# Half-array products of two heads issued in turns, each head to its own bank, in a hybrid transformer block

## The chip, the cores and the metric

One core of one Trainium2 chip runs the whole program in one launch. The metric is the device time of one execution in microseconds (us); the kernel before has a median of 3474.94 us over three runs (3471.09 to 3478.48).

## The reference, cut to what matters

512 tokens of width 1024, all in float32. A first block of two layers, each: gated feed-forward, a mixer, gated feed-forward. A second block of two layers: gated linear attention (GLA) or sparse attention (NSA), each with a convolutional feed-forward. The change touches three places:

```
def _rwkv7_scan(r, w, k, v, kk, a):          # mixer, 6 heads of 64
    def step(state, inp):
        sa = jnp.einsum('bhij,bhj->bhi', state, a_t)
        state = state * w_t + sa * b_t + v_t * k_t
        y_t = jnp.einsum('bhij,bhj->bhi', state, r_t)
...
def _dilated_attention(q, k, v, slopes, window, dilation):   # mixer, 6 heads of 64
    s = jnp.einsum('bnqchd,bnkchd->bnqchk', qb, kb)
    s = jnp.where(valid, s + bias, -jnp.inf)
    p = jnp.exp(s - logsumexp(s));  o = einsum(p, vb)
...
# GLA, 4 heads with keys of 64: score of a query t and a key s is
#   sum over c of q[t,c] * k[s,c] * exp(sum of the log gates of c from s+1 to t)
```

The mixer joins RWKV, dilated attention and a convolution over 31 taps, and projects the result with `w_out`.

## The kernel before

A projection (`gemm`, lines 261 to 272) multiplies 128 output features by 512 tokens: 8 blocks of the inner width, three TensorE products each (high by high, high by low, low by high), 24 products of 128x512 into one bank. `load_w` brings the weights (SP queue), ACT makes the high part (L258), DVE the low part (L259).

Heads go in pairs: two heads of 64 stand in the lower and the upper 64 partitions of a tile, so a product over the 64 channels of one head uses 64 rows of the array. A product of float32 is written to the queue once and shows in the trace as two records.

PSUM is handed out by name, in the program's order of allocation (`BANKS`):

```
BANKS = {"mm": 2, "rr": 1, "rx": 1, "rz": 1, "at": 2, "po": 1}
```

"mm" serves the projections of the mixer from the seventh on. A tile of a name waits until the tile that had its buffer is read out. The mixer (`mixer`) drives seven generators, `r0` to `r2` (RWKV pairs, with the banks rr, rz and rx), `a0` to `a2` (dilated pairs, bank at) and `c` (the convolution, bank mm), by the list `MIXER`, which lets `c`, `a0`, `a1`, `a2` make all their allocations up to their ends in part before `r0` reaches its scores; then it lets `mem_kv` (8 projections to 256 tokens, bank mm) follow as `tail`. A scheduler of the framework then sets each engine's order from dependences and priorities; the engines run their orders strictly one after the other.

An RWKV pair (`rwkv_pair`): projections, gates, then the scores (L572: for each head, two tiles of four 128x128 products, masked by DVE to SA and SR at L574 and L575), a DMA of SA to DRAM and back (L576, L584), a solve of 15 steps on POOL (L615, L616), a copy (L617), DMAs out and back (L618, L628), the matrices ZD (L634), pM (L637), three iterations (L649, L650), W (L657), G (L666), H (L672), a scan of 7 chunks (L683, L684), the output (L690, L693), the group norm (L696 to L706), transposes (L712) and the gate (L716 to L718). The key transposes are L622.

A dilated pair (`dilated_pair`, `causal_pair`): four query blocks i = 3 to 0, for each head one product of 64x(128(i+1)) (L799), softmax (L731, L732), transposes (L743), products with the values (L749).

GLA (`gla_pair`): for two heads, four diagonal score blocks (L1024), then nine levels with four (two in level 7) products of 128x128 per head (L1047), merged by DVE (L1050) or copied by ACT (L1053). `stream_pair` (NSA) shares `causal_pair`.

Of the kernel before, what the change touches and what calls it, by code (L numbers as in the profile page):

```python
# [13 lines left out]
AF = mybir.ActivationFunctionType  # L14
OP = mybir.AluOpType
# [3 lines left out]
T = 512  # L19
# [167 lines left out]
class Net:  # L187
# [306 lines left out]
    def rwkv_pair(self, l, i, win, xs, R, shared, out):  # L494
# [24 lines left out]
        a = self.s([128, T], "rate")  # L519
# [23 lines left out]
        AR = [self.s([128, 4, 2, 64], "AR") for _ in range(2)]  # L543
        BK = [self.s([128, 4, 2, 64], "BK") for _ in range(2)]
# [20 lines left out]
        SA = [self.s([128, 8, 64], "SA") for _ in range(2)]  # L565
        SR = [self.s([128, 8, 64], "SR") for _ in range(2)]
        wide = lambda name: self.c(name).unsqueeze(1).broadcast_to((128, 4, 64))
        for h in range(2):
            for u in range(2):
                p = self.ps([128, 4, 2, 64])  # L570
                for j in range(4):
                    self.T.matmul(p[:, j].rearrange("p a t -> p (a t)"), BK[u][hb[h], j].rearrange("p a t -> p (a t)"),  # L572
                                  AR[u][hb[h], j].rearrange("p a t -> p (a t)"), start=True, stop=True)
                self.V.tensor_tensor(SA[h][:, h4[u]], p[:, :, 0], wide("strict"), OP.mult)  # L574
                self.V.tensor_tensor(SR[h][:, h4[u]], p[:, :, 1], wide("incl"), OP.mult)  # L575
            self.S.dma_start(dN[h], SA[h][hb[h]])  # L576
        yield

# [17 lines left out]
        for u in range(2):  # L596
            p = self.ps([128, 4, 128])
            for j in range(4):
                n = 4 * u + j
# [16 lines left out]
            self.G.tensor_tensor(Z[:, 0, 0:t, t:16], Z[:, 0, 0:t, t:16], tmp[:, 0:t, 0:nt], OP.add)  # L616
        self.V.tensor_copy(Z[:, 1], Z[:, 0].rearrange("p r t -> p t r"))  # L617
        self.S.dma_start(dZ, Z)  # L618
        for h in range(2):
            pB = self.ps([128, 8, 64])  # L620
            for n in range(8):
                self.T.transpose(pB[:, n], BK[n // 4][hb[h], n % 4].rearrange("p a t -> p (a t)"), self.ident[hb[h], hb[h]])  # L622
            self.A.activation(Bt[h], pB, AF.Copy)
        yield
        C2 = self.s([128, 2, 8, 16], "C2")
        for w in range(2):
# [108 lines left out]
    def causal_pair(self, score, V, tables, z, po, heap):  # L735


        def second(i, P):
            PT = []
            for h in range(2):  # L740
                pt = self.ps([128, (i + 1) * 128])
                for b in range(i + 1):
                    self.T.transpose(pt[:, b * 128:(b + 1) * 128], P[h][:, b * 128:(b + 1) * 128], self.ident)  # L743
                t = self.s([128, (i + 1) * 128], "sm_pt", heap=heap)
                self.A.activation(t, pt, AF.Copy)
                PT.append(t)
            for b in range(i + 1):
                for h in range(2):
                    self.T.matmul(po[64 * h:64 * h + 64, i * 128:(i + 1) * 128], V(h, b), PT[h][:, b * 128:(b + 1) * 128],  # L749
                                  start=b == 0, stop=b == i)  # L750

        tab = [self.s([128, T], "tab", heap=heap) for _ in range(2)]
        for h in range(2):
            self.S.dma_start(tab[h], tables[h])
        last = None
        for i in (3, 2, 1, 0):
            n = (i + 1) * 128
            P = []
            for h in range(2):
                ps = self.ps([128, n])  # L760
                score(ps, h, i)
                P.append(self.softmax(ps, tab[h][:, T - n:T], n, z[:, i, h:h + 1], heap))
            if last:
                second(*last)
            last = i, P
            yield
        second(*last)
        yield

    def dilated_pair(self, l, i, win, xs, R, out):  # L770

        qkv = []
        for w in range(3):
            ps = self.proj(win[10 + 3 * w + i], xs)
            f = self.s([128, T], "aq")
            self.V.tensor_tensor(f, ps, R, OP.mult)
            qkv.append(f)
        q, k, f = qkv
        yield
        pss = self.ps([128, 4, 4])  # L780
        for w in range(2):
            sq = self.s([128, T], "asq", heap="ap")
# [12 lines left out]
        yield  # L795

        def score(ps, h, i):
            b = slice(64 * h, 64 * h + 64)
            self.T.matmul(ps, q[b, i * 128:(i + 1) * 128], k[b, 0:(i + 1) * 128], start=True, stop=True)  # L799
# [197 lines left out]
    def gla_pair(self, i, win, xs, R, low, mk, Vk, rr, out):  # L997
# [19 lines left out]
        self.V.tensor_tensor(k, ps, R, OP.mult)  # L1017
        yield
        S = [self.s([128, 4, 128], "gS") for _ in range(2)]
        for h in range(2):  # L1020
            p = self.ps([128, 4, 128])
            for j in range(4):
                tj = slice(j * 128, (j + 1) * 128)
                self.T.matmul(p[:, j], k[hb[h], tj], q[hb[h], tj], start=True, stop=True)  # L1024
            self.V.tensor_tensor(S[h], p, self.ident.unsqueeze(1).broadcast_to((128, 4, 128)), OP.mult)
        far = [[None, None], [None, None]]
        for lv in range(9):
            n = 1 << lv
            eq = self.s([128, T], "geq")
            self.A.activation(eq, g, AF.Exp)  # L1030
            self.V.tensor_tensor(eq, eq, q, OP.mult)
            if lv == 0:
                ek = k
            else:
                gv = g.rearrange("p (b c) -> p b c", c=n)
                ek = self.s([128, T], "gek")
                self.G.tensor_tensor(ek.rearrange("p (b c) -> p b c", c=n), gv[:, :, n - 1:n].broadcast_to((128, T // n, n)), gv, OP.subtract)
                self.A.activation(ek, ek, AF.Exp)
                self.V.tensor_tensor(ek, ek, k, OP.mult)
            if lv < 8:  # L1040
                gw = g.rearrange("p (b w c) -> p b w c", w=2, c=n)
                self.V.tensor_tensor(gw[:, :, 1], gw[:, :, 1], gw[:, :, 0, n - 1:n].broadcast_to((128, T // (2 * n), n)), OP.add)
            for h in range(2):
                pairs = {7: ((0, 1), (2, 3)), 8: ((0, 2), (0, 3), (1, 2), (1, 3))}.get(lv, ((0, 0), (1, 1), (2, 2), (3, 3)))
                p = self.ps([128, len(pairs), 128])
                for u, (s, t) in enumerate(pairs):
                    self.T.matmul(p[:, u], ek[hb[h], s * 128:(s + 1) * 128], eq[hb[h], t * 128:(t + 1) * 128], start=True, stop=True)  # L1047
                if lv < 7:
                    m = mk[lv // 4][:, (lv % 4) * 128:(lv % 4 + 1) * 128].bitcast(I32)
                    self.V.copy_predicated(S[h], m.unsqueeze(1).broadcast_to((128, 4, 128)), p)  # L1050
                else:
                    far[h][lv - 7] = self.s([128, len(pairs), 128], "gfar")
                    self.A.activation(far[h][lv - 7], p, AF.Copy)  # L1053
            yield
        for h in range(2):
            hd = 2 * i + h
# [200 lines left out]
    def stream_pair(self, u, st, q, K, V, gates, O, bank):  # L1257
# [3 lines left out]
        po = self.ps([128, T], bank)  # L1261
        g = u // 2

        def score(ps, h, i):
            for w in range(2):
                self.T.matmul(ps, q[h][:, i * 128:(i + 1) * 128], K[g][w][:, 0:(i + 1) * 128], start=w == 0, stop=w == 1)
# [245 lines left out]
```

## Time and profile before

| what | value |
|---|---|
| median of three runs | 3474.94 us |
| the profiled execution | 3467.64 us |
| its span, first to last instruction | 3464.6 us |
| TensorE (PE) busy | 3419.1 us, 99% of the span |
| VectorE (DVE) busy | 1748.7 us, 50% |
| ScalarE (ACT) busy | 1232.1 us, 36% |
| GpSimd (POOL) busy | 538.8 us, 16% |
| mean granted TensorE clock | 0.996 of full speed |

The profiled execution stands 3.0 us above its span and 7.3 us below the median. PE's busy time counts a product until its modelled end, so the spacing of starts, and not the mean duration, tells what one costs.

### The profile page before, as it was taken

To read this page: it belongs to the slowest core of one execution; us is meant where nothing else is said; L and a number is where in the kernel's file an instruction comes from. 1 tells how busy PE (TensorE), PEld (TensorE's weight loads), DVE (VectorE), ACT (ScalarE), POOL (GpSimd) and SP (SyncE) were. 2 spreads that over 40 slices of the span, in tenths; PEclk is the share of its full clock that TensorE was granted. 3 is DMA by queue.
4 is the path that set the end of the run, shared out by engine and by line. 5 is a ranking of instruction groups with operands and counts; after the bars stand their busy time and mean duration, and the time that the engine had idled before them with its cause. 6 is when DMAs were issued, how large, how long until landed. Compare 5 with 4: busy or idle time off the path is not lost.

```text
span 3464.6 us, 43276 instructions
## 1 busy us (share of the span) xinstructions
PE 3419.1 (99%) x17126; PEld 2729.0 (79%) x17126; DVE 1748.7 (50%) x2857; ACT 1232.1 (36%) x1946; POOL 538.8 (16%) x509
## 2 busy tenths in 40 slices
PE   8999999999999999999999999999999999999998
PEld 6888777878888888877778888777888887778886
DVE  5333498663333433359765333385655354465532
ACT  3222334442222322233444222343433244643332
POOL 2110025011111111012401110020211000211100
PEclk9999999999999999999999999999999999999999
DMA  4223322132233223322123223322322333132232
GB/s 138 94 92 109 101 85 64 40 126 95 94 91 98 91 97 93 109 94 78 54 96 106 94 95 103 110 68 70 107 92 96 106 121 97 49 98 94 97 91 80
DMA packets 127593, 321.55 MB, mean 93 GB/s; under 512 B 32384, under 2 KB 34976, under 8 KB 127392
## 3 DMA queue, kind: packets, MB, share of 16 engines
q1 hardware_dynamic: 127392, 318.80, 29.0%
q8 instruction: 134, 2.20, 0.3%
q14 instruction: 67, 0.55, 0.0%
HBM read 303.81 MB, written 14.94 MB: 92 GB/s over the span
## 4 chain that ended last, share of the span: by engine, by line
PE 94%; DVE 3%; POOL 1%; DMA 1%; issue 1%; ACT 0%; SPq 0%; DVEq 0%; POOLq 0%; ACTq 0%
PE mm L272 13%; PE mm L270 13%; PE mm L271 13%; PE at L271 8%; PE at L270 8%; PE at L272 8%; PE rr L272 4%; PE rr L271 4%; PE rr L270 4%; PE rx L272 3%; PE rx L270 3%; PE rx L271 3%; PE po L749 1%; PE at L799 1%; PE at L743 1%
## 5 line engine op out<-in xcount | busy, mean ns | idle before, releaser
L258 ACT ACTIVATE whi<-raw 128x1024 fp32r<-128x1024 f32 (+2 forms) x566 | 562.6, 995 | 1685.2 <-issue 528.8
L259 DVE TENSOR_TENSOR wlo<-raw,whi 128x1024 fp32r<-128x1024 f32 (+2 forms) x566 | 650.7, 1150 | 502.0 <-ACT whi L258 486.2
L270 PE MATMUL mm<-xh,whi 128*128 128x512 f32 x1216 | 485.1, 399 | 9.1 <-ACT whi L258 9.0
L272 PE MATMUL mm<-xh,wlo 128*128 128x512 f32 x1216 | 487.5, 401 | 0.0
L271 PE MATMUL mm<-xl,whi 128*128 128x512 f32 x1216 | 484.7, 399 | 0.8 <-DVE xl L347 0.7
L272 PE MATMUL at<-xh,wlo 128*128 128x512 f32 x736 | 291.3, 396 | 0.0
L270 PE MATMUL at<-xh,whi 128*128 128x512 f32 x736 | 291.1, 395 | 0.0
L271 PE MATMUL at<-xl,whi 128*128 128x512 f32 x736 | 291.0, 395 | 0.0
L373 POOL TENSOR_TENSOR fg<-fg,bR 128x512 f32<-128x512 f32 x88 | 155.2, 1765 | 806.6 <-ACT fg L372 806.6
L270 PEld LDWEIGHTS mm<-xh,whi 128*128 128x128 f32 x1216 | 228.9, 188 | 65.1 <-ACT whi L258 9.5
L272 PEld LDWEIGHTS mm<-xh,wlo 128*128 128x128 f32 x1216 | 228.7, 188 | 60.6 <-issue 3.9
L271 PEld LDWEIGHTS mm<-xl,whi 128*128 128x128 f32 x1216 | 228.7, 188 | 57.3 <-issue 2.5
L270 PE MATMUL mm<-hi,whi 128*128 128x512 f32 x652 | 259.8, 400 | 3.3 <-ACT hi L287 1.5
L271 PE MATMUL mm<-lo,whi 128*128 128x512 f32 x652 | 258.2, 396 | 0.1
L272 PE MATMUL mm<-hi,wlo 128*128 128x512 f32 x652 | 257.5, 396 | 0.0
L331 POOL TENSOR_TENSOR nacc<-nacc,nsq 128x512 f32<-128x512 f32 x70 | 107.0, 1529 | 781.3 <-ACT nsq L330 780.8
L272 PEld LDWEIGHTS at<-xh,wlo 128*128 128x128 f32 x736 | 138.1, 188 | 35.5 <-DVE wl L514 1.5
L271 PEld LDWEIGHTS at<-xl,whi 128*128 128x128 f32 x736 | 138.2, 188 | 34.8 <-issue 1.5
L272 PE MATMUL rr<-xh,wlo 128*128 128x512 f32 x416 | 164.8, 396 | 0.8 <-DVE wlo L259 0.8
L270 PEld LDWEIGHTS at<-xh,whi 128*128 128x128 f32 x736 | 138.2, 188 | 34.1 <-ACT gy L1005 0.8
L271 PE MATMUL rr<-xl,whi 128*128 128x512 f32 x416 | 164.3, 395 | 0.0
L270 PE MATMUL rr<-xh,whi 128*128 128x512 f32 x416 | 164.2, 395 | 0.0
(667 smaller groups left out, 5878.8 us busy)
## 6 DMA issues: line engine op xcount, KB each, us to landing
raw<-ffn_gu SPq DMA_DIRECT2D x176, 512.0 KB
raw<-c_gu SPq DMA_DIRECT2D x88, 512.0 KB
raw<-ffn_dn SPq DMA_DIRECT2D x64, 448.0 KB
raw<-w_in SPq DMA_DIRECT2D x46, 512.0 KB
raw<-ffn_dn SPq DMA_DIRECT2D x32, 512.0 KB
raw<-c_dn SPq DMA_DIRECT2D x32, 448.0 KB
raw<-a_w_in SPq DMA_DIRECT2D x17, 512.0 KB
park<-x SPq DMA_DIRECT2D x32, 256.0 KB
```

Source lines behind the costliest of these rows:

```text
L258: self.A.activation(hi, raw, AF.Copy)
L259: self.V.tensor_tensor(lo, raw, hi.bitcast(F32), OP.subtract)
L270: self.T.matmul(ps, wh, xh, start=first and j == 0, stop=False)
L271: self.T.matmul(ps, wh, xl, start=False, stop=False)
L272: self.T.matmul(ps, wl, xh, start=False, stop=last and j == nk - 1)
L331: self.G.tensor_tensor(acc, acc, sq, OP.add)
L373: self.G.tensor_tensor(g, g, R, OP.mult)
L743: self.T.transpose(pt[:, b * 128:(b + 1) * 128], P[h][:, b * 128:(b + 1) * 128], self.ident)
L749: self.T.matmul(po[64 * h:64 * h + 64, i * 128:(i + 1) * 128], V(h, b), PT[h][:, b * 128:(b + 1) * 128], start=b == 0, stop=b == i)
L799: self.T.matmul(ps, q[b, i * 128:(i + 1) * 128], k[b, 0:(i + 1) * 128], start=True, stop=True)
```

## The change

For two heads whose products use the lower and the upper half of the array, the products are now written in turns, head 0, head 1, head 0, head 1, with both output tiles allocated first. RWKV's scores and key transposes take the second head's tile from "mm". The dilated scores are cut into blocks of 128 keys, in turns by head. In `stream_pair` the products keep their order; only the softmax of the first head is now written after both heads' products.

```diff
-        for h in range(2):
-            for u in range(2):
-                p = self.ps([128, 4, 2, 64])
-                for j in range(4):
-                    self.T.matmul(p[:, j]..., BK[u][hb[h], j]..., AR[u][hb[h], j]..., start=True, stop=True)
-                self.V.tensor_tensor(SA[h][:, h4[u]], p[:, :, 0], wide("strict"), OP.mult)
-                self.V.tensor_tensor(SR[h][:, h4[u]], p[:, :, 1], wide("incl"), OP.mult)
+        for u in range(2):
+            p = [self.ps([128, 4, 2, 64]), self.ps([128, 4, 2, 64], "mm")]
+            for j in range(4):
+                for h in range(2):
+                    self.T.matmul(p[h][:, j]..., BK[u][hb[h], j]..., AR[u][hb[h], j]..., start=True, stop=True)
+            for h in range(2):
+                self.V.tensor_tensor(SA[h][:, h4[u]], p[h][:, :, 0], wide("strict"), OP.mult)
+                self.V.tensor_tensor(SR[h][:, h4[u]], p[h][:, :, 1], wide("incl"), OP.mult)
...
+        pB = [self.ps([128, 8, 64]), self.ps([128, 8, 64], "mm")]
+        for n in range(8):
+            for h in range(2):
+                self.T.transpose(pB[h][:, n], BK[n // 4][hb[h], n % 4]..., self.ident[hb[h], hb[h]])
         for h in range(2):
-            pB = self.ps([128, 8, 64])
-            for n in range(8):
-                self.T.transpose(pB[:, n], BK[n // 4][hb[h], n % 4]..., self.ident[hb[h], hb[h]])
-            self.A.activation(Bt[h], pB, AF.Copy)
+            self.A.activation(Bt[h], pB[h], AF.Copy)
...
-            P = []
-            for h in range(2):
-                ps = self.ps([128, n])
-                score(ps, h, i)
-                P.append(self.softmax(ps, tab[h][:, T - n:T], n, z[:, i, h:h + 1], heap))
+            ps = [self.ps([128, n]) for _ in range(2)]
+            score(ps, i)
+            P = [self.softmax(ps[h], tab[h][:, T - n:T], n, z[:, i, h:h + 1], heap) for h in range(2)]
...
+        def score(ps, i):
+            for j in range(i + 1):
+                for h in range(2):
+                    b = slice(64 * h, 64 * h + 64)
+                    self.T.matmul(ps[h][:, j * 128:(j + 1) * 128], q[b, i * 128:(i + 1) * 128], k[b, j * 128:(j + 1) * 128], start=True, stop=True)
...
+        p = [self.ps([128, 4, 128]) for _ in range(2)]
+        for j in range(4):
+            for h in range(2):
+                self.T.matmul(p[h][:, j], k[hb[h], tj], q[hb[h], tj], start=True, stop=True)
...
+            p = [self.ps([128, len(pairs), 128]) for _ in range(2)]
+            for u, (s, t) in enumerate(pairs):
+                for h in range(2):
+                    self.T.matmul(p[h][:, u], ek[hb[h], s * 128:(s + 1) * 128], eq[hb[h], t * 128:(t + 1) * 128], start=True, stop=True)
```

(The calls are shortened with `...` inside; the last two pieces are GLA's diagonal blocks and levels.) Lines move by 3 to 8: the scores are L573 in the changed kernel, the key transposes L625, pM L641, the dilated scores L804, GLA's levels L1053.

How the order moves on PE, at three places. First place, layer 0 of the mixer: the RWKV scores. Before, while a projection (mm_3016, the tile that `c` uses) runs, the first product group of r0's second head stands in the middle of it:

```order
L441 MATMUL rx_4110<-cpack,ksq_4108 128x2 x2
L572 MATMUL rr_3683<-AR_3638,BK_3640 128x128 x4
L271 MATMUL mm_3016<-xl_2467,whi_3012 128x512
L272 MATMUL mm_3016<-xh_2466,wlo_3013 128x512
L270 MATMUL mm_3016<-xh_2470,whi_3012 128x512
```

Changed, the second head's groups of r0 (mm_3681, mm_3695) and of r1 (mm_3987) stand behind the last projection of the mixer's input, mm_3573; these are the rows at its end:

```order
L272 MATMUL mm_3573<-xh_2470,wlo_3570 128x512
L449 MATMUL at_5102<-cpack,hex_5100 128x128 x4
L449 MATMUL at_5110<-cpack,hex_5108 128x128 x4
L596 MATMUL rr_3735<-cpack,AR_3651 64x128 x4
L573 MATMUL mm_3695<-AR_3651,BK_3653 128x128 x4
L625 MATMUL mm_3811<-cpack,BK_3652 128x64 x4
L625 MATMUL mm_3811<-cpack,BK_3653 128x64 x4
L431 MATMUL at_5116<-cpack,aq_3306 128x128 x4
L804 MATMUL at_5129<-aq_3273,aq_3240 128x128 x4
L603 MATMUL rr_3742<-cpack,shq_2685 64x128 x4
L804 MATMUL at_5130<-aq_3273,aq_3240 128x128 x4
L573 MATMUL mm_3987<-AR_3945,BK_3947 128x128 x4
```

The second head's scores moved from the midst of the projections to their end; the key transposes stand with all of one tile in a row (mm_3811), and the dilated scores with the four blocks of one head together (at_5129, later at_5130).

Second place, the end of the same mixer. Before, projections of `mem_kv` (mm_5752, 256 wide) and already those of `w_out` (mm_5817) stand between the last transposes of the RWKV pairs:

```order
L271 MATMUL mm_5752<-ml_5460,whi_5748 128x256
L272 MATMUL mm_5752<-mh_5459,wlo_5749 128x256
L712 MATMUL rx_4977<-cpack,gn_y_4955 64x128 x4
L938 MATMUL mm_5779<-cpack,mvf_5777 128x128 x2
L270 MATMUL mm_5817<-hi_5801,whi_5820 128x512
L271 MATMUL mm_5817<-lo_5802,whi_5820 128x512
```

Changed, the three pairs end together, and nothing stands between the scan's outputs (L697), the transposes (L716), the gates (L720) and the first product of `w_out`:

```order
L697 MATMUL rz_4853<-rS_4676,Rt_3961 64x64
L716 MATMUL rr_4806<-cpack,gn_y_4729 64x128 x4
L716 MATMUL rx_4989<-cpack,gn_y_4967 64x128 x4
L716 MATMUL rr_4813<-cpack,gn_y_4729 64x128 x4
L716 MATMUL rz_4912<-cpack,gn_y_4887 64x128 x4
L716 MATMUL rx_4996<-cpack,gn_y_4967 64x128 x4
L720 MATMUL rr_4820<-lora_u_2571,lora_w_2576 128x512
L716 MATMUL rz_4919<-cpack,gn_y_4887 64x128 x4
L720 MATMUL rx_5003<-lora_u_2571,lora_w_2576 128x512
L720 MATMUL rz_4926<-lora_u_2571,lora_w_2576 128x512
L270 MATMUL mm_5853<-hi_5837,whi_5856 128x512
```

All of `mem_kv` moved ahead of them. Third place, GLA's level 0. Before, four products of one head and then four of the other:

```order
L271 MATMUL at_17164<-xl_16895,whi_17160 128x512
L1047 MATMUL rx_17612<-geq_17608,gk_17080 128x128 x4
L1047 MATMUL rr_17618<-geq_17608,gk_17080 128x128 x4
L272 MATMUL at_17164<-xh_16894,wlo_17161 128x512
L1024 MATMUL at_17632<-gq_17123,gk_17156 128x128 x4
```

Changed:

```order
L1053 MATMUL rx_17684<-geq_17680,gk_17152 128x128
L1053 MATMUL rr_17685<-geq_17680,gk_17152 128x128
L1053 MATMUL rx_17684<-geq_17680,gk_17152 128x128
L1053 MATMUL rr_17685<-geq_17680,gk_17152 128x128
L1053 MATMUL rx_17684<-geq_17680,gk_17152 128x128
L1053 MATMUL rr_17685<-geq_17680,gk_17152 128x128
L1053 MATMUL rx_17684<-geq_17680,gk_17152 128x128
L1053 MATMUL rr_17685<-geq_17680,gk_17152 128x128
```

Here the two heads do stand in turns. From GLA's output projection to the end of the program PE's order is the same in both kernels, and so it is up to the scores of r0 in layer 0.

## Rows read from the trace of the kernel before

**Rows 1.** The page: busy time by engine, and the chain that ended last

```profile
PE 3419.1 (99%) x17126; PEld 2729.0 (79%) x17126; DVE 1748.7 (50%) x2857; ACT 1232.1 (36%) x1946; POOL 538.8 (16%) x509
...
PE 94%; DVE 3%; POOL 1%; DMA 1%; issue 1%; ACT 0%; SPq 0%; DVEq 0%; POOLq 0%; ACTq 0%
```

**Rows 2.** Busy time by stretch: mixer 0, mixer 1, GLA (columns in the first row)

```profile
core 0: us, PE busy (x) PEld busy (x) DVE busy (x) ACT busy (x) POOL busy (x), PEclk, DMA share, GB/s
...
545.00:708.00 163.00, 156.70 (x1521) 129.45 (x1519) 114.10 (x287) 70.89 (x164) 39.12 (x72) 0.98 0.22 63
1650.00:1814.00 164.00, 157.75 (x1531) 129.29 (x1530) 117.58 (x292) 71.59 (x166) 39.38 (x72) 0.99 0.23 67
2240.00:2400.00 160.00, 157.32 (x867) 123.61 (x866) 116.39 (x208) 75.72 (x137) 29.32 (x24) 0.99 0.21 69
```

**Rows 3.** Timeline of PE: start, us, engine, line, operation, count

```profile
462.25 1.16 PE L572 MATMUL rr<-AR,BK 64*128 64x128 f32 x8
463.33 0.49 PE L272 MATMUL mm<-xh,wlo 128*128 128x512 f32 x1
463.66 0.40 PE L270 MATMUL mm<-xh,whi 128*128 128x512 f32 x1
463.90 0.39 PE L271 MATMUL mm<-xl,whi 128*128 128x512 f32 x1
```

**Rows 4.** Timeline of PE in GLA: two heads' blocks, rx and rr

```profile
2258.18 0.27 PE L1024 MATMUL rx<-gq,gk 64*128 64x128 f32 x1
2258.28 0.27 PE L1024 MATMUL rr<-gq,gk 64*128 64x128 f32 x1
2258.29 0.27 PE L1024 MATMUL rx<-gq,gk 64*128 64x128 f32 x1
```

**Rows 5.** Timeline of PE: r0's third score group, where the two orders part

```profile
477.74 1.16 PE L572 MATMUL rr<-AR,BK 64*128 64x128 f32 x8
```

**Rows 6.** Timelines of DVE and PE: last SA and first pM of r0, r1, r2

```profile
490.46 0.42 DVE L574 TENSOR_TENSOR SA<-rr,cpack 128x256 f32<-128x256 f32 x1
543.76 1.00 PE L637 MATMUL rr<-No,ZD 128*128 128x64 f32 x8
524.99 0.41 DVE L574 TENSOR_TENSOR SA<-rz,cpack 128x256 f32<-128x256 f32 x1
584.54 1.22 PE L637 MATMUL rz<-No,ZD 128*128 128x64 f32 x10
556.05 0.42 DVE L574 TENSOR_TENSOR SA<-rx,cpack 128x256 f32<-128x256 f32 x1
601.31 0.96 PE L637 MATMUL rx<-No,ZD 128*128 128x64 f32 x7 [2.09 <-DVE ZD L634]
```

**Rows 7.** Timeline of POOL: the solve of r0, its first and last step

```profile
512.51 0.21 POOL L615 TENSOR_TENSOR T<-N,Z 64x15 f32<-64x15 f32 x1
529.19 0.21 POOL L616 TENSOR_TENSOR Z<-Z,T 64x15 f32<-64x15 f32 x1
```

**Rows 8.** Timelines of PE and DVE: small products, and a step of the scan

```profile
692.03 0.29 PE L270 MATMUL mm<-mh,whi 128*128 128x256 f32 x1
692.15 0.28 PE L271 MATMUL mm<-ml,whi 128*128 128x256 f32 x1
645.09 0.74 PE L666 MATMUL rx<-BKt,W 64*64 64x64 f32 x18
645.77 1.12 PE L799 MATMUL at<-aq,aq 64*128 64x512 f32 x2
638.26 0.28 DVE L684 TENSOR_SCALAR rS<-rz,ec 128x64 f32<-128x64 f32 x1 [0.35 <-PE rz L672]
```

**Rows 9.** Timelines of DVE and PE: group norm and gate of r2, w_out beside them

```profile
686.20 0.68 DVE L696 TENSOR_REDUCE gn_m<-rx 128x8 f32<-128x512 f32 x1
705.82 0.75 DVE L718 SCALAR_TENSOR_TENSOR bv<-bv,vec,rx 128x512 f32<-128x512 f32 x1 [1.19 <-PE rx L716]
705.72 0.50 PE L271 MATMUL mm<-lo,whi 128*128 128x512 f32 x1
```

More of the change, by code (lines that the diff above doesn't have):

```diff
@@ L567, in rwkv_pair @@
         wide = lambda name: self.c(name).unsqueeze(1).broadcast_to((128, 4, 64))
-        for h in range(2):
-            for u in range(2):
-                p = self.ps([128, 4, 2, 64])
-                for j in range(4):
-                    self.T.matmul(p[:, j].rearrange("p a t -> p (a t)"), BK[u][hb[h], j].rearrange("p a t -> p (a t)"),
-                                  AR[u][hb[h], j].rearrange("p a t -> p (a t)"), start=True, stop=True)
-                self.V.tensor_tensor(SA[h][:, h4[u]], p[:, :, 0], wide("strict"), OP.mult)
-                self.V.tensor_tensor(SR[h][:, h4[u]], p[:, :, 1], wide("incl"), OP.mult)
+        for u in range(2):
+            p = [self.ps([128, 4, 2, 64]), self.ps([128, 4, 2, 64], "mm")]
+            for j in range(4):
+                for h in range(2):
+                    self.T.matmul(p[h][:, j].rearrange("p a t -> p (a t)"), BK[u][hb[h], j].rearrange("p a t -> p (a t)"),
+                                  AR[u][hb[h], j].rearrange("p a t -> p (a t)"), start=True, stop=True)
+            for h in range(2):
+                self.V.tensor_tensor(SA[h][:, h4[u]], p[h][:, :, 0], wide("strict"), OP.mult)
+                self.V.tensor_tensor(SR[h][:, h4[u]], p[h][:, :, 1], wide("incl"), OP.mult)
+        for h in range(2):
             self.S.dma_start(dN[h], SA[h][hb[h]])
@@ L618, in rwkv_pair @@
         self.S.dma_start(dZ, Z)
+        pB = [self.ps([128, 8, 64]), self.ps([128, 8, 64], "mm")]
+        for n in range(8):
+            for h in range(2):
+                self.T.transpose(pB[h][:, n], BK[n // 4][hb[h], n % 4].rearrange("p a t -> p (a t)"), self.ident[hb[h], hb[h]])
         for h in range(2):
-            pB = self.ps([128, 8, 64])
-            for n in range(8):
-                self.T.transpose(pB[:, n], BK[n // 4][hb[h], n % 4].rearrange("p a t -> p (a t)"), self.ident[hb[h], hb[h]])
-            self.A.activation(Bt[h], pB, AF.Copy)
+            self.A.activation(Bt[h], pB[h], AF.Copy)
         yield
@@ L795, in dilated_pair @@
         yield
-        def score(ps, h, i):
-            b = slice(64 * h, 64 * h + 64)
-            self.T.matmul(ps, q[b, i * 128:(i + 1) * 128], k[b, 0:(i + 1) * 128], start=True, stop=True)
+        def score(ps, i):
[3 more added lines that the diff above has]
+                    self.T.matmul(ps[h][:, j * 128:(j + 1) * 128], q[b, i * 128:(i + 1) * 128], k[b, j * 128:(j + 1) * 128], start=True, stop=True)
         yield from self.causal_pair(score, lambda h, b: Vk[:, b, 64 * h:64 * h + 64],
@@ L1019, in gla_pair @@
         S = [self.s([128, 4, 128], "gS") for _ in range(2)]
-        for h in range(2):
[L1021 to L1025, printed above, removed]
+        p = [self.ps([128, 4, 128]) for _ in range(2)]
+        for j in range(4):
+            for h in range(2):
+                tj = slice(j * 128, (j + 1) * 128)
+                self.T.matmul(p[h][:, j], k[hb[h], tj], q[hb[h], tj], start=True, stop=True)
+        for h in range(2):
+            self.V.tensor_tensor(S[h], p[h], self.ident.unsqueeze(1).broadcast_to((128, 4, 128)), OP.mult)
         far = [[None, None], [None, None]]
@@ L1042, in gla_pair @@
                 self.V.tensor_tensor(gw[:, :, 1], gw[:, :, 1], gw[:, :, 0, n - 1:n].broadcast_to((128, T // (2 * n), n)), OP.add)
+            pairs = {7: ((0, 1), (2, 3)), 8: ((0, 2), (0, 3), (1, 2), (1, 3))}.get(lv, ((0, 0), (1, 1), (2, 2), (3, 3)))
+            p = [self.ps([128, len(pairs), 128]) for _ in range(2)]
+            for u, (s, t) in enumerate(pairs):
+                for h in range(2):
+                    self.T.matmul(p[h][:, u], ek[hb[h], s * 128:(s + 1) * 128], eq[hb[h], t * 128:(t + 1) * 128], start=True, stop=True)
             for h in range(2):
[L1044 to L1047, printed above, removed]
                 if lv < 7:
                     m = mk[lv // 4][:, (lv % 4) * 128:(lv % 4 + 1) * 128].bitcast(I32)
-                    self.V.copy_predicated(S[h], m.unsqueeze(1).broadcast_to((128, 4, 128)), p)
+                    self.V.copy_predicated(S[h], m.unsqueeze(1).broadcast_to((128, 4, 128)), p[h])
                 else:
                     far[h][lv - 7] = self.s([128, len(pairs), 128], "gfar")
-                    self.A.activation(far[h][lv - 7], p, AF.Copy)
+                    self.A.activation(far[h][lv - 7], p[h], AF.Copy)
             yield
@@ L1262, in stream_pair, with score @@
         g = u // 2
-        def score(ps, h, i):
-            for w in range(2):
-                self.T.matmul(ps, q[h][:, i * 128:(i + 1) * 128], K[g][w][:, 0:(i + 1) * 128], start=w == 0, stop=w == 1)
+        def score(ps, i):
+            for h in range(2):
+                for w in range(2):
+                    self.T.matmul(ps[h], q[h][:, i * 128:(i + 1) * 128], K[g][w][:, 0:(i + 1) * 128], start=w == 0, stop=w == 1)
         yield from self.causal_pair(score, lambda h, b: V[:, b, 64 * g:64 * g + 64],
```

## The prediction, made before the changed kernel was run

> **What bounds the kernel.** I read the page first: TensorE is busy for 99% of the span, and 94% of the chain that ended last runs through it [rows 1]. So whatever saves PE slots saves time, and whatever leaves PE without work that is ready costs time; no other engine is above 50%. The windows say where there is room: the second half of each mixer leaves PE idle for 163.00 - 156.70 = 6.3 us and 164.00 - 157.75 = 6.25 us, GLA for 160.00 - 157.32 = 2.7 us [rows 2]. In the mixers that density comes from cover: the RWKV pairs run one behind the other, and projections and `mem_kv` fill PE while a pair waits for its solve.
>
> **What a slot costs.** PE's timelines give spacings of starts. A projection product starts 0.24 us after the last one [rows 3]; 0.23 over longer runs of them, which I use. A `mem_kv` product, 256 wide, takes 0.12 [rows 8]. A float32 product leaves two records, and of 128 columns in half the array each takes 0.11: the next rx block starts 0.11 us after the one before [rows 4]. Eight such records keep the projection away for 463.33 - 462.25 = 1.08 us [rows 3], so some 0.1 to 0.2 us of each group is the change of shape; I take 0.1. A 64x64 product takes 0.06 (18 records in 645.77 - 645.09 = 0.68 us, two to a product) [rows 8].
>
> **GLA: the part that does what it says.** The order puts the levels and the diagonal blocks in turns, both banks, rr and rx, being GLA's own. There are 19 pairs of groups of up to 16 records (304 in all: 272 in the levels, 32 on the diagonal). That halves share time is seen already: rr starts at 2258.28 and rx at 2258.29, 0.01 us apart, where a slot is 0.11 [rows 4]. There the program has four products of rx and then four of rr; the last three records of the first head run beside the first three of the second. So a pair of adjacent groups costs 13 slots today, and groups with something between them 16. By the order 10 of the 19 are adjacent: 10 x 13 + 9 x 16 = 274 slots against 19 x 8 = 152. The 122 slots at 0.11 are 13.4 us, and 9 changes of shape less are 0.9: **-14 us**. GLA is 157 of 160 us PE [rows 2], so most of it should reach the end; the bounds are -10 (DVE's merges between levels become the wait; DVE is 116 of 160) and -17. The Trainium skill, "TensorE: Matmul & The Clock Gate", section Part 3: Packing small matmuls, says that matmuls start and end strictly in program order. The overlap above, of a later group with an earlier one, is against it; by that rule all 19 pairs would cost 16 slots now, and GLA would gain 17 us.
>
> **The mixers: the part that doesn't.** In the rows of the changed order, RWKV scores, key transposes and dilated scores still stand grouped by head. The second head's tile comes from "mm" (or is the second "at"), and that tile is not free when the first head's is. "mm" is handed out in the program's order, and the list `MIXER` lets `c` and the dilated pairs allocate ahead of `r0`'s scores. So r0's second head waits for the mixer's last projections, and with it those of r1 and r2: all three solves start late and together. The Trainium skill, "TensorEngine Tiling (Array Packing)", section Gotcha 1: PSUM Pressure, warns of the cause: row tiles must go to different banks. No run here shows that rule by itself, and my sum does not use it.
>
> The path through layer 0, from r0's third score group at 477.74 [rows 5], where the orders part:
>
> 1. To the last input projection the changed order has 332 products: 211 of 512 columns at 0.23 make 49 us; 88 of 128 columns at 0.22, 34 smaller ones and some 20 changes of shape make 26. That is 75 us.
> 2. To r2's second-head scores it has 171: 11 projections (2.5), 91 of 128 (20), 69 smaller (6.5), changes (3): 32 us. So 477.74 + 75 + 32 = 585; I add 4 for waits on DVE's masks and take 589 (585 to 595).
> 3. From the last SA to the first pM (two trips through DRAM, POOL's 15 steps, ZD) the pairs took 53.3, 59.5 and 45.3 us [rows 6]; I take the mean, 53, so pM at 642. The low bound is the fastest. The high one is 66: POOL's loop alone takes 529.19 - 512.51 + 0.21 = 16.9 us [rows 7], the three loops now stand step by step in turns in POOL's order, r2's first step is behind most of r0's and r1's, and SP has r0's last DMAs behind r2's.
> 4. From pM to `w_out` the order has: iterations of all three pairs with the `mem_kv` left (147 products at 0.12 = 18 us, 115 of 128 at 0.22 = 25, smaller ones 9), 52 us and 3 of waits; the scan, 7 chunks, each a product, a step of DVE of 0.28 us after a wait of 0.35 [rows 8], a mask and the way back, some 1 us: 7; 138 products of 64x64 at 0.06: 8; then group norm and gate, with nothing beside them on PE. That took 705.82 + 0.75 - 686.20 = 20.4 us for r2 alone [rows 9]; the three pairs share DVE, so 23 (20 to 29). Together 93 us: **`w_out` starts at 735**.
>
> Before, the end of r2's gate was at 706.57, but 14 products of `w_out` had already run beside it, until 705.72 [rows 9]: the like mark is 705.72 - 14 x 0.23 = 702.5. Layer 0 so loses **32 us** (bounds +14 and +60 from steps 2 to 4). Layer 1 has the same order of things, with the second heads' scores a little earlier against `mem_kv` (86 products after pM, not 151; 65 x 0.12 = 8 us less): **+24 us** (+6 to +52). What is late next is `w_out` and all behind it; from there the orders are alike, and weights for `w_out` stand on SP behind the Z transfers and the stores of `mem_kv`, tens of us ahead of need, so I give them nothing.
>
> The same from the other side: idle. PE's work stays, less 4 to 6 us of shape changes per layer. If the start of the solves leaves 5 us uncovered, the solve 20 (the `mem_kv` before pM covers little of 53), the scan 5 and the group norm 15, a mixer idles 45 us against 6.3 now [rows 2]: +39, less 5, +34. The two ways agree within a few us.
>
> **Small edits.** Dilated scores in blocks: two records of 512 columns end after 1.12 us [rows 8], eight of 128 after 1.16 [rows 3], so 0.04 for each of 30 such products: +1 us, hidden in the above. `stream_pair`'s later softmax: its order on PE is unchanged; nothing (-1 to +1, by GLA's 2.7 us of idle as the nearest like stretch).
>
> **Sum:** +32 + 24 - 14 = **+42 us**. The sum is made on the profiled execution (3467.64, 3.0 above its span); the median is 7.3 above that. I add it to the median: 3474.94 + 42 = **3517 us**.
>
> **Rivals.**
>
> *A. Everything goes in turns as written.* Then L572 (6 pairs, 32 records each; half of 192 slots at 0.11 is 11 us), the transposes (half of 192 at 0.03: 3) and the dilated scores (6 pairs, 10 blocks, 2 heads, 2 records; half at 0.11: 13) are saved too: -41 in all, **3434**. Against it: the order shows none of the three in turns. Chance 0.03.
>
> *B. The delay of the solves is hidden, faster.* If each solve finishes with its cover still running, only GLA counts: -14, **3461**. For it: POOL, SP and ACT have slack [rows 1]. Against it: it decides at a solve shorter than the work in front of pM, and the order has 40 `mem_kv` products there, 5 us, and some 25 us of other work, against 53 [rows 6]. Chance 0.05.
>
> *C. The three solves get in each other's way.* If POOL's loops run one after another behind r2's start, two more loops of 16.9 us [rows 7] come in front of pM, some 25 us after what overlaps, in each layer: 3517 + 50 = **3567**. Chance 0.13. For it: the loops stand step by step in turns.
>
> *D. About even.* Losses at their low bounds (14 + 6) and GLA's gain: within 10 us of before, **3480**. Chance 0.1, the half of it within 0.2%.
>
> The forecast has 0.69. A measurement of this kernel can tell about 0.2%, 7 us. Faster by more: A, B, a little of D, 0.07; within: 0.06; slower: 0.87. The range leaves out A and B and the far end of C: 3474 to 3572.
>
> **What would show it.** In the profile after: idle of 35 to 60 us in each mixer on PE, released by POOL's ZD (L637 in the changed numbering), by DVE in the scan (L687) and in the group norm; r2's last SA near 589 and the first product of `w_out` near 735; starts of rx and rr within 0.01 us all through L1053, GLA some 14 us shorter; scores at L573 not in turns. It is wrong if idle in the mixers stays below 15 us, or if PE runs L573 or L804 in turns after all.

## The result, and the profile after

The changed kernel takes 3503.22 us (median of four runs, 3498.31 to 3504.49) against 3476.71 for the kernel before, run beside it. The medians stand 26.5 us apart; the ratio is 1.0086, 95% interval 1.0072 to 1.0099, which is some 30 us. Below, differences between whole runs go by the ratios, and differences between stages by the profiles. Forecast were +42 us, a range of 3474 to 3572, and 0.87 for slower. The sign, the place and GLA's gain in the middle of a loss came as forecast; the sizes of three terms did not.

The page of the changed kernel, the rows that answer to [rows 1]:

```profile
PE 3426.5 (98%) x17270; PEld 2750.0 (79%) x17270; DVE 1733.6 (49%) x2857; ACT 1228.0 (35%) x1946; POOL 506.0 (14%) x509
...
PE 94%; DVE 4%; ACT 1%; issue 1%; POOL 0%; DMA 0%; SPq 0%; DVEq 0%; POOLq 0%; ACTq 0%
```

The mean granted clock fell from 0.996 to 0.985. Both kernels have long runs of projections in the same order, so the time can be laid out by stage: from the first input projection of a mixer to the first projection of the feed-forward behind it, and likewise for GLA and NSA. First the kernel before, then the changed one; the rows are mixer 0, mixer 1 and GLA, and the first column behind the stretch is its length.

```profile
core 0: us, PE busy (x) PEld busy (x) DVE busy (x) ACT busy (x) POOL busy (x), PEclk, DMA share, GB/s
384.46:748.19 363.73, 356.87 (x2471) 283.43 (x2470) 271.54 (x580) 151.67 (x290) 82.74 (x126) 0.99 0.26 78
1490.04:1852.09 362.05, 355.64 (x2471) 281.88 (x2470) 272.39 (x580) 151.40 (x290) 82.92 (x126) 1.00 0.27 81
2223.02:2443.26 220.24, 215.71 (x1113) 169.54 (x1112) 146.96 (x261) 97.82 (x170) 38.07 (x31) 0.99 0.24 78
```

```profile
385.14:777.02 391.88, 369.67 (x2543) 300.89 (x2542) 268.98 (x580) 150.86 (x290) 64.78 (x126) 0.93 0.24 72
1518.87:1895.58 376.71, 357.83 (x2543) 293.80 (x2542) 263.28 (x580) 150.51 (x290) 65.70 (x126) 0.95 0.26 78
2266.50:2479.53 213.03, 205.82 (x1113) 159.56 (x1112) 143.21 (x261) 97.23 (x170) 40.44 (x31) 1.00 0.25 81
```

| stage | forecast | measured |
|---|---|---|
| mixer 0 | +32 | 391.88 - 363.73 = +28.2 |
| mixer 1 | +24 | 376.71 - 362.05 = +14.7 |
| GLA | -14 | 213.03 - 220.24 = -7.2 |
| NSA | 0 | 264.75 - 263.22 = +1.5 (in the experiments it is about 263.2 or 264.7 too, whatever was changed; the longer ones have 3.4 us more at the lower level of the clock) |

The rest is +0.6; together 37.8 us, the difference of the two spans (3502.4 and 3464.6). The profiled execution of before was one of its quicker ones, 7 to 9 us under its medians, so the medians stand less apart. Part of GLA's gain is the clock and not the change. Experiment 6, which leaves GLA alone, ran it at the full clock throughout:

```profile
2250.68:2469.36 218.68, 214.15 (x1114) 168.42 (x1113) 147.00 (x261) 97.62 (x170) 38.09 (x31) 1.00 0.24 79
```

The kernel before has 3.4 us at the lower level in GLA, the changed one none, so like with like the gain is 218.68 - 213.03 = 5.65 us.

What PE waits for in mixer 0, before and then changed, the longest waits (us in total, times, longest):

```profile
PE at L449 <- DVE hex L446: 3.1, 1, 3.1
PE rx L637 <- DVE ZD L634: 2.1, 1, 2.1
```

```profile
PE rr L716 <- POOL gn_y L710: 9.3, 1, 9.3
PE at L748 <- DVE sm_m L735: 3.1, 1, 3.1
PE at L804 <- DVE aq L794: 1.5, 1, 1.5
PE at L441 <- ACT asq L786: 1.3, 1, 1.3
```

The group norm of all three pairs now stands in the open, 9.3 us. But PE's idle time grew only from 363.73 - 356.87 = 6.9 to 391.88 - 369.67 = 22.2 us, 15 of the 28. The rest is in the granted clock, 0.99 and now 0.93. The timeline of the changed kernel's PE shows what that is: `mem_kv` products, 256 wide, ahead of the first pM.

```profile
630.71 0.41 PE L271 MATMUL mm<-ml,whi 128*128 128x256 f32 x1
630.93 0.41 PE L272 MATMUL mm<-mh,wlo 128*128 128x256 f32 x1
...
633.41 0.28 PE L270 MATMUL mm<-mh,whi 128*128 128x256 f32 x1
633.53 0.28 PE L271 MATMUL mm<-ml,whi 128*128 128x256 f32 x1
```

The same product starts every 0.21 us up to 632.85 and every 0.12 from there on: the two levels of the clock, 1.2 and 2.4 GHz. Added up over windows of 1 us, mixer 0 has 54.6 us at the lower level against 6.8 before, and mixer 1 has 34.1 against 3.4. Half of mixer 0's lies in one stretch, in which PE is busy for most of the time:

```profile
605.70:633.00 27.30, 21.37 (x96) 18.32 (x97) 19.72 (x57) 9.63 (x19) 13.76 (x33) 0.50 0.27 48
```

### The profile page after: what moved, and what is told of

It is laid out like the page before. It is cut to its first block, busy times and chain, and to the rows that moved or that the text cites. A ratio compares the mean times of both kernels' runs of the same rounds, so it can differ in the third digit from the quotient of the medians.

```text
span 3502.4 us, 43586 instructions
## 1 busy us (share of the span) xinstructions
PE 3426.5 (98%) x17270; PEld 2750.0 (79%) x17270; DVE 1733.6 (49%) x2857; ACT 1228.0 (35%) x1946; POOL 506.0 (14%) x509
## 4 chain that ended last, share of the span: by engine, by line
PE 94%; DVE 4%; ACT 1%; issue 1%; POOL 0%; DMA 0%; SPq 0%; DVEq 0%; POOLq 0%; ACTq 0%
PE mm L270 13%; PE mm L272 13%; PE mm L271 13%; PE at L271 8%; PE at L270 8%; PE at L272 7%; PE rr L271 4%; PE rr L272 4%; PE rr L270 4%; PE rx L270 3%; PE rx L271 3%; PE rx L272 3%; PE po L754 1%; PE at L804 1%; PE at L748 1%
```

## The experiments

Theory after the result: the second heads' tiles from "mm" make the three solves late and let the three pairs end together; GLA's gain stands by itself; the dilated edit does little. Ratios are against the kernel before, run beside each.

**1. GLA alone** (the last two pieces of the diff in the kernel before).

> The kernel before with the change to GLA alone (diagonal blocks and levels in turns by head). Theory, from the profile after: GLA keeps its gain by itself, about 7 us, so 3470 against 3477, and nothing moves elsewhere. Rival 1, the prediction's term of 14 us: the gain is 14 and the profile after shows only half of it because something late from the mixers eats the rest; then 3463. Rival 2: GLA is not bound by PE and gains nothing, 3477.

3467.48 us, ratio 0.9978 (0.9968 to 0.9987): -8 us, and its GLA is 213.07 us long, as in the changed kernel. The rival of 14 us falls. (That GLA stage, too, has no time at the lower level, so 1.6 us of its gain are the clock, as said above.) What the profile of the changed kernel shows of the missing half: level 0 stands in turns, rx and rr 0.01 us apart, and its 16 records take 1.1 us; but the diagonal blocks of the second pair, whose two tiles come from at, still stand head by head, 8 records in each.

```profile
2306.72 1.16 PE L1029 MATMUL at<-gq,gk 64*128 64x128 f32 x8
...
2309.40 0.37 PE L1053 MATMUL rx<-geq,gk 64*128 64x128 f32 x1
2309.41 0.37 PE L1053 MATMUL rr<-geq,gk 64*128 64x128 f32 x1
2309.62 0.27 PE L1053 MATMUL rx<-geq,gk 64*128 64x128 f32 x1
2309.62 0.27 PE L1053 MATMUL rr<-geq,gk 64*128 64x128 f32 x1
...
2310.92 1.16 PE L1029 MATMUL at<-gq,gk 64*128 64x128 f32 x8
...
2337.29 0.44 PE L979 MATMUL rz<-cpack,mem_p 128*128 128x128 f32 x2 [1.14 <-POOL mem_p L972]
```

From group to next start, the 304 records took 34.8 us before and 28.4 now, in 26 unbroken groups each, and 2.3 of these are two new waits for POOL's mem_p (1.2 and 1.1), one of them in the last row. So the products gained 8.7, the waits took 2.3 back.

**2. The RWKV part alone** (scores and key transposes).

> The kernel before with the change to the RWKV scores and key transposes alone. Theory: all of the loss in the two mixers is here, because the second head's tile comes from mm and the solves start late: +43 us in the profiled stretches (28 and 15), so about 3512 to 3520. Rival: the loss is shared with the dilated scores, whose two heads now hold both at buffers; then this alone costs no more than +25.

3505.46 us, ratio 1.0091 (1.0077 to 1.0106): +32 us; its mixers are 382.52 and 380.19 us long. The loss is here, though smaller than the 43 expected. The rival, that the dilated scores share in it and this alone costs at most 25, is out, if not by much: the interval starts at 27.

**3. The dilated part alone** (blocks in turns, later softmax).

> The kernel before with the change to the dilated scores (blocks of 128 keys in turns) and the later softmax of stream_pair alone. Theory: two records of 512 columns become eight of 128 at nearly the same cost, and the heads still stand one behind the other: 0 to +4 us, 3477 to 3481. Rival: holding both at buffers before the first softmax makes the dilated chain late: +10 us or more, 3487. Rival of the change's own text: half of the score slots are saved, -13 us.

3461.18 us, ratio 0.9962 (0.9949 to 0.9975): -13 us. The theory was wrong. The number of the change's own text, half of the slots, is met, but not its reason: in the trace the scores stand head by head (eight records in 1.08 us, then the other eight) and take 16.7 us in mixer 0 where they took 15.1. What is gone is idle time and the low clock: its mixers are 360.66 and 360.65 us long with 2.7 us of idle each, and have 3.4 us at the lower level.

**4. The bank alone.** All products by head, as before; only the tile is taken elsewhere:

```diff
-                p = self.ps([128, 4, 2, 64])
+                p = self.ps([128, 4, 2, 64], "mm" if h else None)
```

> The kernel before, with its RWKV scores still written by head, one head after the other; only the tile of the second head is taken from mm instead of the pair's own bank. No product is put in turns, key transposes are as before. Theory: the bank alone does it, as in the run with the whole RWKV change: +35 to +45 us. Rival: writing in turns by itself delays the solves (the first head's matrix waits for the second): then this costs under 10 us.

3510.41 us, ratio 1.0103 (1.0088 to 1.0118): +36 us. One argument, the name of the bank, does all of it; writing in turns has no part in the loss.

**5. GLA and the dilated part, RWKV undone.**

> The changed kernel with its RWKV part undone (scores and key transposes as before). Theory: the gains of GLA (7 us) and of the dilated part (13 us, e3) add up, since they lie in different stretches: -18 to -21 against before, about 3455. Rival: the dilated part's gain is only a luckier course of the mixer and goes with any other change: then -7 to -10.

3455.47 us, ratio 0.9952 (0.9940 to 0.9965): -17 us. The gains add up to most of their sum (21). This version beats both kernels. In the changed kernel the dilated gain is not seen: its mixers (768.6 us together) are no shorter than those of the RWKV part alone (762.7).

**6. A bank that is free.** Second heads of r0 and r1 from rx, in turns; r2 as before:

```diff
+        alt = ("rx", "rx", None)[i]
...
+                p = [self.ps([128, 4, 2, 64]), self.ps([128, 4, 2, 64], alt)]
...
```

> The kernel before with the RWKV scores of r0 and r1 in turns, the second head's tile from rx, the bank of r2, which stands idle then; r2's scores as before. Theory: with a bank that is free the solves of r0 and r1 aren't late, and the loss of 31 us is gone; one of two groups per pair stands in turns by the order, about 1.1 us saved for each of four pairs, while r2 loses time on its own bank: -4 to +6. Rival: it is not the bank's lateness but the form of the code (both heads' matrices are masked and sent out together), then +20 or more.

3494.43 us, ratio 1.0061 (1.0048 to 1.0073): +21 us, the rival's number, but not by the rival's cause. The matrices of r0 and r1 are out earlier than before (r0's last SA at 471.21, where [rows 6] have 490.46). It is r2 that is late: its own bank has been lent, its last scores start at 592.93 and no longer at 554.21. The expectation took r2's loss for small. That it is all of the result fits the scores, which are earlier for r0 and r1, but no run has it apart. In both cases a bank that looks idle is wanted by the next tile in the program's order.

**7 and 8. One pair late.** As experiment 4, for one pair alone (`"mm" if h and i == 2`, then `i == 0`).

> The kernel before with only r2's second head on mm, all scores by head. Theory 1 (cover): the loss comes from three pairs that end together with nothing beside them; with r0 and r1 on time it is under a third of e4's +36: +4 to +12. Theory 2 (lateness of the last solve): r2's solve sets the end of the mixer by itself, and this costs nearly as much as e4: +25 or more.

> The kernel before with only r0's second head on mm, all scores by head. Theory 1 (cover): r0's work can no longer stand beside the others' solves: +5 to +15. Theory 2 (lateness of the last solve): r0 is not last, so -2 to +4.

r2 late: 3486.57 us, ratio 1.0042 (1.0029 to 1.0054), +15. r0 late: 3506.54, ratio 1.0104 (1.0087 to 1.0121), +36, as much as all three. Theory 1 (cover) names the reason, but its sizes (4 to 12 and 5 to 15) are too small in both. Theory 2 has it the wrong way round: the last SA comes at 588.49 with r2 late and at 573.13 with r0 late, and the earlier one costs more. What differs is how the pairs end. DVE's first step of the group norm in mixer 0, r2 late:

```profile
671.29 0.69 DVE L696 TENSOR_REDUCE gn_m<-rr 128x8 f32<-128x512 f32 x1 [1.90 <-PE rr L693]
688.38 0.69 DVE L696 TENSOR_REDUCE gn_m<-rz 128x8 f32<-128x512 f32 x1 [1.21 <-PE rz L693]
704.91 0.68 DVE L696 TENSOR_REDUCE gn_m<-rx 128x8 f32<-128x512 f32 x1
```

and r0 late, in mixer 0 and then in mixer 1:

```profile
692.20 0.69 DVE L696 TENSOR_REDUCE gn_m<-rz 128x8 f32<-128x512 f32 x1 [0.36 <-PE rx L693]
692.81 0.68 DVE L696 TENSOR_REDUCE gn_m<-rx 128x8 f32<-128x512 f32 x1
695.74 0.68 DVE L696 TENSOR_REDUCE gn_m<-rr 128x8 f32<-128x512 f32 x1
...
1820.41 0.69 DVE L696 TENSOR_REDUCE gn_m<-rx 128x8 f32<-128x512 f32 x1 [6.86 <-PE rz L693]
1821.02 0.68 DVE L696 TENSOR_REDUCE gn_m<-rz 128x8 f32<-128x512 f32 x1
1821.62 0.68 DVE L696 TENSOR_REDUCE gn_m<-rr 128x8 f32<-128x512 f32 x1
```

With r2 late the pairs end 17 us apart, like a staircase; with r0 late they end within 4 and then within 1.2 us, as in the changed kernel (711.09, 711.70, 712.29). The table sets this beside what it costs, mixer 0 and then mixer 1, in the profiled executions. A pair's end is its first step of the group norm, counted from the start of the mixer; idle is PE's.

| run | pairs end apart by | last pair later by | mixer longer by | idle | at the lower level |
|---|---|---|---|---|---|
| before | 7, 9; 7, 9 | | | 6.9; 6.4 | 6.8; 3.4 |
| 7, r2 late | 17, 17; 21, 23 | 18.2; 19.0 | 8.4; 10.9 | 5.0; 6.4 | 20.5; 23.9 |
| 6, rx lent | 29, 32; 24, 42 | 31.3; 32.4 | 11.6; 15.6 | 7.3; 6.9 | 17.1; 30.7 |
| 8, r0 late | 1, 3; 1, 1 | 8.9; 19.6 | 11.3; 25.6 | 11.6; 17.2 | 17.1; 41.0 |
| changed kernel | 1, 1; 1, 1 | 25.4; 10.5 | 28.2; 14.7 | 22.2; 18.9 | 54.6; 34.1 |

Where the pairs end apart, a third to three fifths of the last one's lateness is lost, and PE idles hardly more than before: one pair's products run beside another's solve and group norm. Where they end together, all of it is lost and some more, and PE idles. So cover decides how much a delay costs. A staircase alone is no remedy: experiment 6 has the widest steps and loses 21 us, and what its mixers and those of experiment 7 lose lies with PE recorded busy, for a good part at the lower clock.

**9 and 10. The dilated part, halved.** First both tiles and both products ahead of the first softmax, uncut; then each head's products cut in blocks of 128 keys, one head after the other:

```diff
-            self.T.matmul(ps, q[b, i * 128:(i + 1) * 128], k[b, 0:(i + 1) * 128], start=True, stop=True)
+            for j in range(i + 1):
+                self.T.matmul(ps[:, j * 128:(j + 1) * 128], q[b, i * 128:(i + 1) * 128], k[b, j * 128:(j + 1) * 128], start=True, stop=True)
```

> The kernel before with one half of the dilated change: both heads' tiles are allocated and both products written before the first softmax, the products uncut (128(i+1) keys in one). In e3 the scores still stood by head and cost 1.6 us more per mixer, yet the mixers were shorter, with 2.7 us of idle PE against 6.9 and 6.4. Theory: the gain is in the order that follows from allocating both tiles first: -8 to -15. Rival: the cutting into blocks lets RWKV's half-array products slip between them; then this gives -3 to +3 and e10 has the gain.

> The kernel before with the other half of the dilated change: the scores of each head cut into blocks of 128 keys, one head after the other, tiles and softmax as before. Theory (see e9): -3 to +4. Rival: -8 to -15, as e3.

Tiles first: 3474.30 us, ratio 1.0003 (0.9993 to 1.0013). Blocks: 3460.91, ratio 0.9968 (0.9956 to 0.9981), -11 us. The rival holds: the cutting has the gain. Its mixers:

```profile
384.49:743.65 359.16, 356.33 (x2543) 289.05 (x2542) 270.41 (x580) 152.38 (x290) 80.21 (x126) 1.00 0.26 79
1485.50:1846.14 360.64, 357.95 (x2543) 290.21 (x2542) 271.69 (x580) 152.43 (x290) 79.66 (x126) 1.00 0.27 82
```

Idle 2.8 and 2.7 us, and nothing and 3.4 us at the lower level. Against the profiled execution of before that is 4.6 and 1.4 us; the rest of the 11 is that the kernel before loses more in most of its executions. Run beside experiment 10 it spreads from 3467.4, at a mean granted clock of 0.996, to 3479.3, at 0.992; the runs of experiment 10 lie between 3460.6 and 3461.5, all at 0.997. Experiment 1, whose mixers are those of before, shows what such an execution has in it, in its second mixer, 367.67 us long where before has 362.05:

```profile
1706.00:1722.00 16.00, 16.00 (x90) 12.91 (x89) 8.93 (x28) 5.85 (x15) 1.27 (x1) 0.57 0.06 23
```

PE is busy for all of 16 us and mostly at the lower level. A wait of 1.42 us for ZD lies ahead of it; the kernel before has the same wait there, 1.32 us, and keeps the full clock. Why cutting the scores takes the two waits and this stretch away was not tried apart: the cut products lie between RWKV's half-array products in the order, but that they cause it is only argued.

**11. Useless work in the group norm, in po.** Eight products of 128x512 per mixer, from the squares of r2's group norm, their result unused:

```diff
+        if i == 2:
+            fill = self.ps([128, T], "po")
+            for _ in range(8):
+                self.T.matmul(fill, self.ident, sq.rearrange("p n t -> p (n t)"), start=True, stop=True)
```

> The changed kernel with 8 useless products of 128x512 float32 in each mixer, from the squares of r2's group norm into the bank po, which nobody uses then: about 7 us of PE work in the 9.3 us in which PE waits for the group norm. Theory, that the granted clock falls because PE runs dry: the granted clock of the stretch after the group norm is full, the transposes and gates behind it take their 0.11 us a record, and the time is 2 to 6 us less, although work was added. Rival: the clock falls for another reason (all three engines' load, the DMA): it stays at half there, and the time is the same or up to 7 us longer per mixer.

3532.56 us, ratio 1.0172 (1.0158 to 1.0186), some 30 us more than the change. As a test of the clock it is spoilt, and it shows the first mechanism once more: in the program's order the filling takes "po" ahead of the last dilated pair, whose scores and products now follow the group norm.

**12. The same in r2's own bank**, four products (`self.ps([128, T])`).

> The changed kernel with 4 useless products of 128x512 float32 in each mixer, from the squares of r2's group norm into r2's own bank rx, ahead of its transposes (e11 took po, and by that moved the last dilated pair behind the group norm). PE's order is otherwise that of the changed kernel. Theory, that the granted clock falls because PE has little to do: behind the filled stretch the transposes' groups of four start about 0.45 us apart and not 0.9 to 1.0, some 3 us less per mixer, against 1 to 2 us by which the filling itself is late: the time within 5 us of the changed kernel's 3503, the clock full from the second transposes on. Rival, that the clock there falls whatever PE does: the groups stay 0.9 to 1.0 us apart, and the time is 2 to 6 us longer.

3511.31 us, ratio 1.0124 (1.0108 to 1.0141): 8 us above the change by the medians, 13 by the ratios. Behind the filling the clock did what the theory says: in mixer 0 it is at the lower level for the first part of the filling, 710.8 to 714.2, and full from there to 727.8. First the changed kernel, then this one, 715 to 725 us in mixer 0:

```profile
715.00:725.00 10.00, 4.46 (x20) 2.98 (x20) 5.20 (x40) 3.50 (x10) 3.04 (x3) 0.50 0.00 0
```

```profile
715.00:725.00 10.00, 8.13 (x35) 3.75 (x33) 4.85 (x9) 6.81 (x16) 3.05 (x3) 1.00 0.00 0
```

Groups of transposes that follow each other start 0.46 us apart, not 1.00:

```profile
720.53 1.06 PE L716 MATMUL rr<-cpack,gn_y 128*64 128x128 f32 x4 [9.33 <-POOL gn_y L710]
721.53 1.06 PE L716 MATMUL rx<-cpack,gn_y 128*64 128x128 f32 x4
```

```profile
718.20 0.63 PE L720 MATMUL rz<-cpack,gn_y 128*64 128x128 f32 x4 [0.38 <-POOL gn_y L714]
718.66 0.60 PE L720 MATMUL rr<-cpack,gn_y 128*64 128x128 f32 x4
```

Mixer 0 is 389.85 us long, 2.0 less than in the changed kernel although work was added. The total misses the expectation: mixer 1 is 385.97, 9.3 more, with a stretch at the lower level from 1731 to 1758 that lies ahead of the filling there, where the changed kernel had one from 1732 to 1749. PE was busy throughout it:

```profile
1731.40:1758.70 27.30, 27.14 (x133) 24.00 (x133) 15.76 (x61) 10.83 (x23) 13.86 (x32) 0.50 0.25 47
```

What lengthened it stays open.

Not tried: both heads' scores in turns into one bank. Two row halves would write the same bank with nothing between them that orders the writes, and whether that is safe is not shown by any run here.

## Why the prediction was right in sign, and where it was off

**The mechanism** held. That nothing in the mixers but the allocation of "mm" moved the solves was read from the order, and experiment 4 shows it: +36 us with no product moved on purpose. Rival A (everything in turns), rival B (the delay hidden) and rival D (about even) are out, and so is C: POOL's steps of three pairs stood in turns, and ZD of all three was done at 622.89 + 6.68 = 629.6, 36 us after the last SA.

```profile
593.52 0.42 DVE L576 TENSOR_TENSOR SA<-mm,cpack 128x256 f32<-128x256 f32 x1 [0.42 <-PE mm L573]
```

```profile
622.89 6.68 POOL L638 TENSOR_TENSOR ZD<-C,cpack 128x512 f32<-128x512 f32 x6 [9.02 <-DMA C<-dZ]
```

```profile
638.69 1.22 PE L641 MATMUL rx<-No,ZD 128*128 128x64 f32 x10
729.41 0.73 PE L270 MATMUL mm<-hi,whi 128*128 128x512 f32 x2
```

**The path through layer 0.** Steps 1 and 2: last SA at 589, measured 593.5. Step 3: pM at 642, measured 638.7, but not by the 53 us of a solve: from the last SA to pM it was 45.2, the solve was ready after 36, and PE reached pM 9 us later, being still at work on what stands ahead, until 633 at the lower clock. That +32 came so near to +28.2 is in part luck: a solve taken too long stood in for work at half clock that the sum did not hold. Step 4: 93 us from pM to `w_out`, measured 729.41 - 638.69 = 90.7, the group norm and gate among them about 20.6 (711.09 to 731.7), forecast 23. `w_out` at 735, measured 729.4. (The bounds of steps 2 to 4 give +17 and +57 for the layer, not +14 and +60; nothing hangs on it.)

**The cross-check failed, though it agreed.** It took idle time for all of the loss, 45 us of it in a mixer. Measured are 22.2 and 18.9 us, and PE waits for ZD nowhere in the two mixers. What it called the uncovered solve was mostly not idle: PE worked through it at half clock, busy for 21.4 of the 27.3 us from 605.7 to 633. Of mixer 0's +28.2, idle time is 15.4. Of the 54.6 us at the lower level PE is busy for 43, before for 6; these 37 us more cost up to 18.5. Together that is 34, some 6 more than the 28.2. Small products of three pairs, standing together, run beside each other and give 4 of them back (from start to next start, the 144 records of the iterations take 15.9 us and not 20.0). In the prediction no term for the clock stood at all, although [rows 2] showed 0.98 and 0.99 in just these stretches: that was the step left out.

**Layer 1** was the mis-sized term: +24, measured +14.7. The +24 took 8 us off layer 0 for `mem_kv`; the trace has 13.5 between the two. Of these 2.9 are idle time, and up to 7.6 are the clock: 34 us at the lower level in place of 55, 25 of them with PE busy in place of 43.

**GLA** was mis-sized at -14, measured -7.2, or some -5.6 with the clock alike. The count of 152 slots took every pair of heads to stand in turns (there are 20 pairs of groups and not 19, two of them of 8 records; the 304 records are right); with the changes of shape at 0.2 a group taken off, the 26.1 us of products are 20.9 / 0.112 = 187 slots. Where both tiles come from at, one frees after the other, and the heads still run apart in part. The number of unbroken groups did not fall either (26 in both). The waits for mem_p were not foreseen; the low bound, -10, looked for DVE's merges instead. The Trainium skill, "TensorE: Matmul & The Clock Gate", section Part 3: Packing small matmuls, has matmuls start strictly in program order, which would have made it -17; the overlap of groups written one after the other, seen before the run, spoke against that, and the measured gain is on the trace's side and below it.

**The dilated part** stood under the small edits at +1 us. Its slots cost 1.6 us more in mixer 0, as said; the -13 by itself lies in waits and a clock that the sum did not hold, and why the cutting removes them stays open. The forecast did not suffer, as in the changed kernel that gain is not seen.

## What to carry to other kernels

A second tile for work done in turns must come from a bank that is free at that point of the program's order of allocation, not one that is idle on the chip: "mm", rx and po were each idle at some time and each made a chain late. Chains that end apart cover each other; look first at whether a change makes them end together, as here a late first chain, which then ended with the others, cost more (+36) than a late last one (+15). And where a stretch runs out of work, sum its granted clock beside its idle time: the stretches at the lower level with PE busy cost about as much here as the idle time. The clock also changes stages that no edit touched, so compare a stage with like clock before a gain is ascribed to the edit.

## What the runs showed of the hardware

- At several places the granted clock fell where PE's work thinned out, and what still ran there took nearly twice as long: in the changed kernel `mem_kv` products start 0.21 us apart and then 0.12. Around one 3.1 us wait in the kernel before:

```profile
560.00:566.00 6.00, 6.00 (x53) 4.70 (x51) 2.54 (x4) 4.26 (x11) 5.01 (x14) 1.00 0.04 4
566.00:569.00 3.00, 0.19 (x4) 0.00 (x0) 3.00 (x4) 0.50 (x1) 2.92 (x1) 0.94 0.21 44
569.00:572.00 3.00, 2.73 (x13) 2.69 (x14) 1.70 (x4) 1.51 (x3) 0.00 (x0) 0.50 0.73 191
```

  Behind useless products in such a gap the clock was full again (experiment 12). Idle time alone is not the whole condition: in experiment 1 a stretch of 16 us at 0.57 and in experiment 12 one of 27.3 us at 0.50 have PE busy throughout, and the same wait of 1.3 to 1.4 us was followed by a low clock in experiment 1 and by the full clock in the kernel before.
- The spread of a kernel's runs can be the clock: the kernel before, run beside experiment 10, takes from 3467.4 us at a mean granted clock of 0.996 to 3479.3 at 0.992. The kernels with the fullest mixers spread less but not alike, experiment 10 over 0.9 us, 3 over 2.4 and 5 over 5.6, and experiment 2, with 18 and 19 us of idle time in its mixers, over 1.5. So full mixers alone do not explain a small spread.
